# A two-layer encoder step: which MLP work runs plain, where the residual lives, and when the down operands are asked for

## The chip, the core and the metric

The kernel runs on one core of one Trainium2 chip. The core has a matrix engine (TensorE, PE in the profile), three other compute engines (VectorE or DVE, ScalarE or ACT, GpSimd or POOL), a sync engine (SP) from whose queue nearly all of this kernel's transfers are issued, and 16 DMA engines that carry them out. The metric is device time in microseconds (us) of one execution.

## The reference

The reference is one inference step of a two-layer encoder over 1024 prompt tokens and 32 sample tokens, 1056 rows of width 1024. Layer 0 mixes with a matrix memory, layer 1 with banded attention; each layer ends with the same kind of MLP. The change touches only what follows attention in layer 1:

```
x = layer_norm(ALPHA * x + (1 + g1) * y, ...)          # y: attention, projected
u = x * (1 + sc2) + sh2
f = square(relu(u @ w_up)) @ w_down                     # 1024 -> 4096 -> 1024
x = layer_norm(ALPHA * x + (1 + g2) * f, ...)
```

Everything is float32. The kernel carries each operand as a high and a low part and adds three products (high x high, high x low, low x high), so every matrix product costs three matmuls for each block of 128 inner rows. Making such a pair (`split`, line 90 with its cast on line 89) takes a cast on ScalarE and a subtraction on VectorE.

## The kernel before

Layer 1's MLP is `mlp7`, lines 1124 to 1515. The 1056 tokens are four quarters of 264 (`QN`). Two quarters make a token pair `tp`; `L.pairs` is (1, 0), so `tp0`, the first, is pair 1. The 4096 hidden columns are 16 groups of 256, here called pairs `pb`.

**Up, plain.** For the pairs listed in `FIRST` (10 to 15) the up product of the first token pair is made in the plain way: `up_tile` (24 matmuls of 264 columns, four of them, 96 in all, for a pair). Their weights come through `raw_up` transfers into a ring of three raw tiles and are split into `w_up`. The first three pairs run while the norm after attention still delivers the tokens, the other three behind them. When a pair's four tiles are done, pairs 14 and 15 go through `h_forms`; pairs 10 to 13 are only stored (`hraw`), and `late` reads them back and forms them later, in pieces laid beside the jobs.

**Up, seven products.** All other (pair, token pair) combinations, 26 of them, are jobs of `Seven`: seven products of 12 matmuls, 84 instead of 96, as in Strassen's scheme with Winograd's sums. They need seven weight forms (`forms`: 11 VectorE operations and 7 ScalarE casts of 128x512, made from two `rdn_u` loads) and moving forms of u (`tforms`: t1 and t2 in the TF tiles, t3 in `ext` and `exu`, T4 over a part of u that is no longer needed). A pair whose two token pairs both run this way (a double) shares its weight forms between two jobs; a pair of `FIRST` has one job only (a single). `seq` in `L1` gives the order: 0, 1, 10, 2, 3, 11, 4, 5, 12, 6, 7, 8, 9, 13, 14, 15.

**H forms.** `h_forms` squares a finished H tile and makes the seven forms that the down product wants: four in HL, three in HM, both single-buffered, stored to DRAM (`hd`). Pairs 14 and 15 are kept plain for the down side and stored to `hpl`.

**Down.** 20 units (five groups of 2 or 3 pairs, four output blocks each) of seven products, with weight forms from `rdn_d` and operands `fx` loaded back from `hd` into free rooms (`Rooms`, `fill`). `fill` asks for all operands for which there are rooms. Rooms come free late: the `ext` tile and half of u when the first token pair's last job is done, the H tiles' memory (the four `f4` tiles) and the rest of u after the last job. Pairs 14 and 15 follow plainly with operands `hs`, loaded from `hpl` into the `f4` tiles (line 1504).

**The residual.** `ACC` is one tile of 8 x 1056 columns. After the norm it is stored to DRAM (`xsp`), the TF tiles take its memory, and `L.reload(0..3)` brings it back in quarters around the end of the jobs; the down product adds into it (line 986).

**What sets the order.** TensorE's instructions in the jobs and the units stand in an order written out by hand (`manual_schedule`; product i of job j sorts by 7j + 2i, so neighbouring jobs interleave). The other engines' orders come from the Tile scheduler; SP's queue is one of them, and a transfer there waits behind any store that waits for its data.

Of the kernel before, what the change touches and what calls it, by code (L numbers as in the profile page):

```python
# [15 lines left out]
P = 128  # L16
# [59 lines left out]
def trunk_kernel(ctx: ExitStack, tc: tile.TileContext, a, o):  # L76
# [7 lines left out]
    def raw_tile(shape, name):  # L84
        return ring.tile(shape, F32, tag="raw", name=name, bufs=3)
# [1038 lines left out]
    def mlp7(L):  # L1124
# [11 lines left out]
        ep = e_cm.__enter__()  # L1136
        hraw = {pb: dr.tile([P, 4, QN], F32, name=f"hraw{l}_{pb}") for pb in L.first if pb < NW}
        hh_cm = tc.tile_pool(name=f"hh{l}", bufs=1, reuse_waits="tile")
# [17 lines left out]
        def h_place(pb, tp):  # L1156
            g = [i for i, (p0, kg) in enumerate(GRP) if p0 <= pb][-1]
            return hd[g][tp][:, :, pb - GRP[g][0]].rearrange("f p l t -> p f (l t)")

        def late(pb, tp):  # L1160

            H = raw_tile([P, 4, QN], f"hl_{l}_{pb}")
            nc.sync.dma_start(H, hraw[pb])
            yield
            dst = h_place(pb, tp)

            def put(f, src):
                t = tmp_t([P, 2, QN], f"hf_{l}_{pb}_{f}", F32R)
                split(t[:, 0], t[:, 1], src)
                nc.sync.dma_start(dst[:, f], t.bitcast(F32).rearrange("p l t -> p (l t)"))  # L1170
            nc.scalar.activation(H, H, AF.Square)
            put(B11, H[:, 1])
            put(B22, H[:, 2])
            yield
            put(B21, H[:, 3])
            nc.vector.tensor_sub(H[:, 1], H[:, 0], H[:, 1])
            nc.vector.tensor_sub(H[:, 0], H[:, 2], H[:, 0])
            put(T1, H[:, 1])
            yield
            nc.vector.tensor_sub(H[:, 2], H[:, 2], H[:, 1])  # L1180
            nc.vector.tensor_sub(H[:, 3], H[:, 3], H[:, 2])
            put(T3, H[:, 0])
            yield
            put(T2, H[:, 2])
            put(T4, H[:, 3])
            yield

# [199 lines left out]
        for j, pb in enumerate(rest):  # L1387
            for f in range(2):
                for q in L.quarters[:2]:
                    up_tile(pb, f, q)  # L1390
                if (j, f) == (0, 1):
                    L.ready(2)
                    tiles = L.scratch()
                    TF.update({(tp, i): tiles[2 * n + i] for n, tp in enumerate(L.pairs) for i in range(2)})
                    exts[tp1] = ring.tile([P, 2, KG, QN], F32R, tag="wc", name=f"exu_{l}", bufs=6)
                    tfs = [tf, tforms(tp1, exts[tp1])]
                if (j, f) == (1, 1):
                    prep(0)
                for n in ((), (0,), (1, 1), (0,), (0, 2), (2, 2))[2 * j + f]:
                    if n < 2:  # L1400
                        next(tfs[n])
# [5 lines left out]
        fx, nfx = {}, {}  # L1407
# [33 lines left out]

        next(tf, None)
        prep(1)
        got[0] = next(preps[0])
        for _ in tfs[1]:
            pass
        lone = max(j for j, (_, tp) in enumerate(jobs) if tp == tp0) + 1
        sevens, lates = {}, list(hraw)
        with tc.manual_schedule(engines={mybir.EngineType.PE}):
            for _, j, i in sorted((7 * j + 2 * i, j, i) for j in range(len(jobs)) for i in range(7)):  # L1450
# [4 lines left out]
                if tp == seq[n][1][-1]:  # L1455
                    advance(n, i)
                elif lates:
                    if i == 0:
                        job = late(lates[0], tp0)
                    if i < 5:  # L1460
                        next(job)
                    if i == 4:
                        del lates[0]
# [10 lines left out]
        for i in range(4):  # L1474
            rooms.add(f4p.tile([P, KG, 2, QN], F32R, tag=f"f4{i}", name=f"fx_4{i}_{l}"))
        for t in L.rooms(tp1):
            rooms.add(t)
        fill(0, fx)
        with tc.manual_schedule(engines={mybir.EngineType.PE}):
            for i, (g, m, phases) in enumerate(units):  # L1480
                more = g + 1 < len(GRP)
                if i < 3:
                    L.reload(i + 1)
                if i == 0:
# [376 lines left out]
    accp = acc_cm1.__enter__()  # L1861
    ACC = accp.tile([P, KC, T], F32, tag="acc", name="ACC")
    acc = {ti: ACC[:, :, t0:t0 + n] for ti, (t0, n) in enumerate(TBS)}
    acc["all"] = ACC
    for ti in rev:
        t0, n = TBS[ti]
        nc.sync.dma_start(acc[ti], xsp[1][:, :, t0:t0 + n])
        more_wo(ti)
# [22 lines left out]
    def end_out1(ti):  # L1891
        t0, n = TBS[ti]
        norms[ti] = flow.add(norm(ti, 2, f"n10_{ti}", W10[ti == rev[-1]], True, lambda ti: nc.sync.dma_start(
            xsp[2][:, :, t0:t0 + n], acc[ti])), now=NOW)
        qo_cm[ti].__exit__(None, None, None)
        if ti == 1:
            open_u2(0)
# [4 lines left out]
    wup1 = {}  # L1902
    FIRST = [10, 11, 12, 13, 14, 15]

# [7 lines left out]
    class L1:  # L1912
# [90 lines left out]
```

## Time and profile before

| | us |
|---|---|
| median of 3 runs | 2505.67 (2505.41 to 2506.22) |
| the profiled execution | 2506.99, its span 2505.2 |
| TensorE busy in the span | 2400.9 (96%) |
| VectorE busy | 1925.2 (77%) |
| ScalarE busy | 1090.4 (44%) |
| mean granted clock of TensorE | 0.980 of full speed |

The profile shows one execution. A row of a group gives line, engine, operation, output and inputs by the program's names, shapes and count, then busy time, the mean of one instruction in ns, and the idle time of the engine just before them with who ended it. The chain of waits is followed back from the last instruction. A table by stage gives the busy time of each engine in a stretch of the span. A timeline gives start and length in us. The up work of layer 1's MLP runs from about 1729 to 2117 us of the span, the down work from there to the end.

### The profile page before, as it was taken

To read this page: it belongs to the slowest core of one execution; us is meant where nothing else is said; L and a number is where in the kernel's file an instruction comes from. 1 tells how busy PE (TensorE), PEld (TensorE's weight loads), DVE (VectorE), ACT (ScalarE), POOL (GpSimd) and SP (SyncE) were. 2 spreads that over 40 slices of the span, in tenths; PEclk is the share of its full clock that TensorE was granted. 3 is DMA by queue.
4 is the path that set the end of the run, shared out by engine and by line. 5 is a ranking of instruction groups with operands and counts; after the bars stand their busy time and mean duration, and the time that the engine had idled before them with its cause. 6 is when DMAs were issued, how large, how long until landed. Compare 5 with 4: busy or idle time off the path is not lost.

```text
span 2505.2 us, 42905 instructions
## 1 busy us (share of the span) xinstructions
PE 2400.9 (96%) x16532; PEld 2307.3 (92%) x16532; DVE 1925.2 (77%) x4368; ACT 1090.4 (44%) x2280; POOL 166.6 (7%) x315
## 2 busy tenths in 40 slices
PE   8999999999999999999999899999978997899997
PEld 4999999999999999999999877799978997799997
DVE  4899999778778768766697766638978877677768
ACT  4544455481221221221375567736666665122212
POOL 0211100000000000000001244400000000000003
PEclk9999999999999999999999999999988999899999
DMA  8433224313223223223123400052567768856631
GB/s 294 120 108 100 83 90 131 99 35 118 93 86 125 93 93 119 93 93 115 59 94 96 101 1 1 25 139 82 167 213 280 262 239 310 326 217 224 234 125 70
DMA packets 248512, 335.29 MB, mean 134 GB/s; under 512 B 13032, under 2 KB 197756, under 8 KB 247284
## 3 DMA queue, kind: packets, MB, share of 16 engines
q1 hardware_dynamic: 248308, 332.55, 39.9%
q8 instruction: 130, 2.13, 0.3%
q14 instruction: 74, 0.61, 0.1%
HBM read 253.47 MB, written 81.40 MB: 134 GB/s over the span
## 4 chain that ended last, share of the span: by engine, by line
PE 74%; DVE 11%; DMA 5%; ACT 3%; issue 2%; POOL 1%; SPq 0%; ACTq 0%; DVEq 0%; POOLq 0%
PE dn L1433 11%; PE up L1333 7%; PE up L118 5%; PE up L119 5%; PE up L120 5%; PE dn L119 5%; PE dn L118 5%; PE dn L120 5%; PE pv L1771 3%; PE s L1714 2%; PE pt L1749 2%; PE o L118 1%; PE o L119 1%; PE o L120 1%; PE op_b L118 1%
## 5 line engine op out<-in xcount | busy, mean ns | idle before, releaser
L1433 PE MATMUL dn<-fx,wf_d 128*128 128x264 f32 x2016 | 257.3, 287 | 17.5 <-DMA fx<-hd 8.4
L1433 PEld LDWEIGHTS dn<-fx,wf_d 128*128 128x128 f32 x2016 | 252.3, 191 | 19.3 <-ACT wf_d L89 8.7
L119 PE MATMUL dn<-h,w_dn 128*128 128x384 f32 (+1 forms) x768 | 249.5, 325 | 0.0
L118 PE MATMUL up<-U,w_up 128*128 128x384 f32 (+1 forms) x768 | 249.2, 325 | 0.0
L119 PE MATMUL up<-U,w_up 128*128 128x384 f32 (+1 forms) x768 | 247.9, 323 | 0.0
L118 PE MATMUL dn<-h,w_dn 128*128 128x384 f32 (+1 forms) x768 | 247.8, 323 | 0.0
L120 PE MATMUL up<-U,w_up 128*128 128x384 f32 (+1 forms) x768 | 247.6, 322 | 0.0
L120 PE MATMUL dn<-h,w_dn 128*128 128x384 f32 (+1 forms) x768 | 247.3, 322 | 0.0
L986 DVE SCALAR_TENSOR_TENSOR ACC<-dn,ada,ACC 128x264 f32<-128x264 f32 (+5 forms) x400 | 160.5, 428 | 72.4 <-PE dn L1433 54.2
L238 DVE SCALAR_TENSOR_TENSOR aacc<-rada,cs,aacc 128x256 f32<-128x256 f32 x448 | 190.8, 481 | 0.0
L1333 PE MATMUL up<-u,wf_u 128*128 128x264 f32 x1248 | 170.5, 291 | 12.2 <-ACT wf_u L89 9.2
L1333 PEld LDWEIGHTS up<-u,wf_u 128*128 128x128 f32 x1248 | 162.4, 194 | 13.2 <-ACT wf_u L89 9.4
L986 DVE SCALAR_TENSOR_TENSOR acc<-dn,ada,acc 128x384 f32<-128x384 f32 (+2 forms) x256 | 119.9, 489 | 48.3 <-PE dn L120 46.7
L1025 ACT ACTIVATE r<-up 128x384 f32<-128x384 f32 (+1 forms) x96 | 44.5, 464 | 246.4 <-PE up L120 236.5
L119 PEld LDWEIGHTS dn<-h,w_dn 128*128 128x128 f32 x768 | 144.5, 188 | 0.2 <-DVE h L1028 0.2
L120 PEld LDWEIGHTS dn<-h,w_dn 128*128 128x128 f32 x768 | 144.5, 188 | 0.0
L120 PEld LDWEIGHTS up<-U,w_up 128*128 128x128 f32 x768 | 144.3, 188 | 0.0
L119 PEld LDWEIGHTS up<-U,w_up 128*128 128x128 f32 x768 | 144.2, 188 | 0.0
L118 PEld LDWEIGHTS up<-U,w_up 128*128 128x128 f32 x768 | 144.2, 188 | 0.1
L118 PEld LDWEIGHTS dn<-h,w_dn 128*128 128x128 f32 x768 | 143.9, 187 | 0.2
L1027 DVE TENSOR_TENSOR r<-r 128x384 f32<-128x384 f32 (+1 forms) x96 | 50.0, 523 | 103.1 <-ACT h L1026 102.5
L1333 PE MATMUL up<-TF,wf_u 128*128 128x264 f32 x624 | 93.2, 301 | 20.3 <-ACT wf_u L89 8.9
(393 smaller groups left out, 6419.9 us busy)
## 6 DMA issues: line engine op xcount, KB each, us to landing
rada<-in_w_ada_dram SPq DMA_DIRECT2D x64, 512.0 KB
hd<-HL SPq DMA_DIRECT2D x24, 1056.0 KB
fx<-hd SPq DMA_DIRECT2D x48, 528.0 KB
raw_up<-in_w_up_dram SPq DMA_DIRECT2D x44, 512.0 KB
hd<-HM SPq DMA_DIRECT2D x24, 792.0 KB
raw_dn<-in_w_down_dram SPq DMA_DIRECT2D x36, 512.0 KB
ada_room<-in_w_ada_dram SPq DMA_DIRECT2D x32, 512.0 KB
rdn_u<-in_w_up_dram SPq DMA_DIRECT2D x32, 512.0 KB
```

The costliest lines, as they stand in the source:

```text
L118: nc.tensor.matmul(ps, wh, mov(0, k), start=(k == 0), stop=False)
L119: nc.tensor.matmul(ps, wh, mov(1, k), start=False, stop=False)
L120: nc.tensor.matmul(ps, wl, mov(0, k), start=False, stop=(k == nk - 1))
L238: nc.vector.scalar_tensor_tensor(acc[:, cnd], raw[:, k], sc, acc[:, cnd], op0=ALU.mult, op1=ALU.add)
L986: nc.vector.scalar_tensor_tensor(xs, ps[:, off + o:off + o + mm_], gate[:, fc, cnd:cnd + 1], xs, op0=ALU.mult, op1=ALU.add)
L1025: nc.scalar.activation(r, ps[:, :n], AF.Relu)
L1027: nc.vector.tensor_mul(r, r, r)
L1333: nc.tensor.matmul(p, self.ws[w][:, wl, k], moving(f, tp, xl, k), start=first and k + n_ == 0, stop=k == 3 and n_ == 2, skip_group_check=n ...
L1433: nc.tensor.matmul(p, ws[w][:, wl, k], t[:, s0, xl], start=first and k + n_ == 0, stop=k == kg - 1 and n_ == 2, skip_group_check=not first)
L1714: nc.tensor.matmul(s[:, b, :w], qst, kk[i][:, g, k0 + j0:k0 + j0 + w], start=(i == 0), stop=(i == 1))
L1749: nc.tensor.transpose(pt[:kp, j - j0, pr * P:(pr + 1) * P], ps_[pr][:, j * P:j * P + kp], ident)
L1771: nc.tensor.matmul(pv[64 * e:64 * e + 64, :nq], V[:kp, vt0 + j, g * 64:(g + 1) * 64], pts[e][:kp, j, :nq], start=(j == 0), stop=(j == nt - 1))
```

## The change

`FIRST` becomes the ten pairs 6 to 15; the jobs of seven products become 22, and `seq` lays doubles and singles alternately: 0, 6, 1, 7, 2, 8, 3, 9, 4, 10, 5, 11, 14, 12, 15, 13. `hraw` and `late` go; every finished plain pair is formed at once by `h_forms`. The steps of `tforms` and of the first weight forms are laid over the longer plain stretch (`at`).

The residual is two tiles of four column blocks each (`acc0`, `acc1`; class `Halves` finds the part asked for), and its transfers are two instead of one. The TF tiles of the first token pair lie in `acc0`, those of the second in `acc1`, and each half is loaded back when its token pair's jobs no longer read it.

`fill` takes a limit: after the first token pair's last job it asks for one operand at products 0, 2 and 4 of each job, and the residual's quarters 0 and 1 are asked for at the ends of two of these jobs, quarter 2 after the last one, quarter 3 at the first unit. For the last two groups the rooms are sorted, so that the fourth group uses the `f4` tiles first and the fifth uses them last.

```diff
-        hraw = {pb: dr.tile([P, 4, QN], F32, ...) for pb in L.first if pb < NW}
-        def late(pb, tp):
-            ...
             if hts[pb, tp][1] == 4:
-                H = hts.pop((pb, tp))[0]
-                if pb in hraw:
-                    nc.sync.dma_start(hraw[pb], H[:, 0:4])
-                else:
-                    h_forms(pb, tp, H)
+                h_forms(pb, tp, hts.pop((pb, tp))[0])
...
-                    tiles = L.scratch()
-                    TF.update({(tp, i): tiles[2 * n + i] for n, tp in enumerate(L.pairs) for i in range(2)})
+                    for n, tp in enumerate(L.pairs):
+                        for i, t in enumerate(L.scratch(n)):
+                            TF[tp, i] = t
...
-                if (j, f) == (1, 1):
+                at = 2 * j + f - 2 * len(rest) + 14
+                if at == 11:
                     prep(0)
-                for n in ((), (0,), (1, 1), (0,), (0, 2), (2, 2))[2 * j + f]:
+                for n in {1: (1,), 2: (1,), 3: (1,), 4: (1,), 5: (1,), 6: (1,), 7: (0,), 8: (0,), 11: (0, 2),
+                          12: (2,), 13: (2, 0)}.get(at, ()):
...
-        def fill(g, into):
+        def fill(g, into, most=99):
             kg = GRP[g][1]
-            while want and len(rooms.free) >= kg:
+            if g >= len(GRP) - 2:
+                rooms.free.sort(key=lambda r: any(r[0] is t for t in f4s) == (g == len(GRP) - 1))
+            while want and len(rooms.free) >= kg and most:
+                most -= 1
                 tp, f = want.pop(0)
...
-                if j == lone - 1 and i == 6:
+                if j == lone and i == 6:
                     rooms.add(ep.tile([P, KG, 2, QN], F32R, tag="e", name=f"fx_e{l}"))
                     for t in L.rooms(tp0):
                         rooms.add(t)
-                    fill(0, fx)
-        L.reload(0)
+                if j > lone + 1:
+                    if i in (0, 2, 4):
+                        fill(0, fx, 1)
+                    elif i == 6 and j < lone + 4:
+                        L.reload(j - lone - 2)
+        L.reload(2)
...
-    ACC = accp.tile([P, KC, T], F32, tag="acc", name="ACC")
+    def acc_half(i, name):
+        return accp.tile([P, 4, T], F32, tag=f"acc{i}", name=f"{name}{i}")
+    def acc_dma(d, x, out=False):
+        for i in range(0, KC, 4):
+            p = [d[:, i:i + 4], x[:, i:i + 4]]
+            nc.sync.dma_start(*(p if out else reversed(p)))
+    acc = {"all": Halves([acc_half(i, "ACC") for i in range(2)])}
...
-    FIRST = [10, 11, 12, 13, 14, 15]
+    FIRST = [6, 7, 8, 9, 10, 11, 12, 13, 14, 15]
-        seq = [(pb, (0,) if pb > 9 else (1, 0)) for pb in (0, 1, 10, 2, 3, 11, 4, 5, 12, 6, 7, 8, 9, 13, 14, 15)]
+        seq = [(pb, (0,) if pb in FIRST else (1, 0)) for pb in (0, 6, 1, 7, 2, 8, 3, 9, 4, 10, 5, 11, 14, 12, 15, 13)]
...
-        def scratch():
-            t = accp.tile([P, 4, 2, KG, QN], F32R, tag="acc", name="TF")
-            return [[t[:, i, hl] for hl in range(2)] for i in range(4)]
+        def scratch(i):
+            t = accp.tile([P, 2, 2, KG, QN], F32R, tag=f"acc{i}", name=f"TF{i}")
+            return [[t[:, n, hl] for hl in range(2)] for n in range(2)]
         def reload(m):
-            if m == 0:
-                acc["all"] = accp.tile([P, KC, T], F32, tag="acc", name="ACC2")
-            nc.sync.dma_start(acc["all"][:, 2 * m:2 * m + 2], xsp[2][:, 2 * m:2 * m + 2])
+            i = m // 2
+            if m % 2 == 0:
+                acc["all"].tiles[i] = acc_half(i, "ACX")
+            k = m % 2 * 2
+            nc.sync.dma_start(acc["all"].tiles[i][:, k:k + 2], xsp[2][:, 4 * i + k:4 * i + k + 2])
```

More of the change, by code (lines that the diff above doesn't have):

```diff
@@ L1136, in mlp7 @@
         ep = e_cm.__enter__()
-        hraw = {pb: dr.tile([P, 4, QN], F32, name=f"hraw{l}_{pb}") for pb in L.first if pb < NW}
         hh_cm = tc.tile_pool(name=f"hh{l}", bufs=1, reuse_waits="tile")
@@ L1158, in h_place @@
             return hd[g][tp][:, :, pb - GRP[g][0]].rearrange("f p l t -> p f (l t)")
-        def late(pb, tp):
[L1162 to L1186, printed above, removed]
         def h_forms(pb, tp, H):
@@ L1439, in unit @@
                         step(i)
-        next(tf, None)
         prep(1)
         got[0] = next(preps[0])
[L1445 to L1448, printed above, removed]
+        lone = max(j for j, (_, tp) in enumerate(jobs) if tp == tp0)
+        sevens = {}
         with tc.manual_schedule(engines={mybir.EngineType.PE}):
@@ L1456, in mlp7 @@
                     advance(n, i)
[L1457 to L1463, printed above, removed]
-                if j == lone - 1 and i == 6:
+                if j == lone and i == 6:
                     rooms.add(ep.tile([P, KG, 2, QN], F32R, tag="e", name=f"fx_e{l}"))
@@ L1473, in mlp7 @@
         f4p = f4_cm.__enter__()
-        for i in range(4):
-            rooms.add(f4p.tile([P, KG, 2, QN], F32R, tag=f"f4{i}", name=f"fx_4{i}_{l}"))
+        f4s += [f4p.tile([P, KG, 2, QN], F32R, tag=f"f4{i}", name=f"fx_4{i}_{l}") for i in range(4)]
+        for t in f4s:
+            rooms.add(t)
         for t in L.rooms(tp1):
@@ L1481, in mlp7 @@
                 more = g + 1 < len(GRP)
-                if i < 3:
-                    L.reload(i + 1)
+                if i == 0:
+                    L.reload(3)
                 if i == 0:
@@ L1861, in trunk_kernel, with __init__, part, __getitem__ @@
     accp = acc_cm1.__enter__()
-    ACC = accp.tile([P, KC, T], F32, tag="acc", name="ACC")
-    acc = {ti: ACC[:, :, t0:t0 + n] for ti, (t0, n) in enumerate(TBS)}
-    acc["all"] = ACC
+    class Halves:
+        def __init__(self, tiles, t0=0, n=T):
+            self.tiles, self.t0, self.n = tiles, t0, n
+        def part(self, t0, n):
+            return Halves(self.tiles, self.t0 + t0, n)
+        def __getitem__(self, at):
+            if at[1] == slice(None):
+                return self.part(at[2].start, at[2].stop - at[2].start)
+            k, t = at[1], at[2] if len(at) > 2 else slice(0, self.n)
+            k0 = k.start if isinstance(k, slice) else k
+            i = k0 // 4
+            k = slice(k0 - 4 * i, k.stop - 4 * i) if isinstance(k, slice) else k - 4 * i
+            return self.tiles[i][:, k, self.t0 + t.start:self.t0 + t.stop]
+    def acc_half(i, name):
[5 more added lines that the diff above has]
+    acc = {"all": Halves([acc_half(i, "ACC") for i in range(2)])}
+    for ti, (t0, n) in enumerate(TBS):
+        acc[ti] = acc["all"].part(t0, n)
     for ti in rev:
         t0, n = TBS[ti]
-        nc.sync.dma_start(acc[ti], xsp[1][:, :, t0:t0 + n])
+        acc_dma(xsp[1][:, :, t0:t0 + n], acc[ti])
         more_wo(ti)
@@ L1892, in end_out1 @@
         t0, n = TBS[ti]
-        norms[ti] = flow.add(norm(ti, 2, f"n10_{ti}", W10[ti == rev[-1]], True, lambda ti: nc.sync.dma_start(
-            xsp[2][:, :, t0:t0 + n], acc[ti])), now=NOW)
+        norms[ti] = flow.add(norm(ti, 2, f"n10_{ti}", W10[ti == rev[-1]], True, lambda ti: acc_dma(
+            xsp[2][:, :, t0:t0 + n], acc[ti], True)), now=NOW)
         qo_cm[ti].__exit__(None, None, None)
```

4 lines of the change are left out of this document (2 added, 2 removed).

## The prediction

> **What bounds the kernel now.** First the page: who fills the span, and the chain of waits.
>
> ```profile
> PE 2400.9 (96%) x16532; PEld 2307.3 (92%) x16532; DVE 1925.2 (77%) x4368; ACT 1090.4 (44%) x2280; POOL 166.6 (7%) x315
> PE 74%; DVE 11%; DMA 5%; ACT 3%; issue 2%; POOL 1%; SPq 0%; ACTq 0%; DVEq 0%; POOLq 0%
> ```
>
> TensorE carries the kernel: an edit is worth what it takes from TensorE's instructions or from its gaps. The gaps near the change show in a table by stage: length, then busy time and instruction count (x) of PE, PEld, DVE, ACT and POOL, the granted clock, DMA share, GB/s.
>
> ```profile
> 1724.00:1807.00 83.00, 77.02 (x610) 76.17 (x609) 78.67 (x114) 58.30 (x102) 0.00 (x0) 0.98 0.47 156
> 1807.00:1850.00 43.00, 29.23 (x185) 28.21 (x186) 31.72 (x48) 19.36 (x35) 0.00 (x0) 0.76 0.51 175
> 1850.00:1940.00 90.00, 82.55 (x621) 80.96 (x620) 75.71 (x142) 64.57 (x118) 0.00 (x0) 0.92 0.78 275
> 1940.00:2090.00 150.00, 150.00 (x1234) 150.00 (x1233) 125.20 (x210) 102.43 (x174) 0.00 (x0) 1.00 0.76 266
> 2090.00:2117.00 27.00, 17.55 (x126) 17.03 (x125) 17.57 (x34) 14.56 (x28) 0.00 (x0) 0.81 0.71 257
> 2117.00:2162.00 45.00, 30.26 (x220) 28.81 (x219) 28.92 (x77) 9.93 (x22) 0.00 (x0) 0.86 1.00 372
> ```
>
> Busy shares mislead here (matmuls overlap and slow down after a gap), so I count matmuls. Their spacing comes from TensorE's timeline, one full job of 84 between two like rows; plain work begins, and down work begins, at the other rows.
>
> ```profile
> 1729.09 0.29 PE L118 MATMUL up<-u,w_up 128*128 128x264 f32 x1
> ...
> 1730.35 0.42 PE L118 MATMUL up<-u,w_up 128*128 128x264 f32 x1
> 1730.57 0.42 PE L119 MATMUL up<-u,w_up 128*128 128x264 f32 x1
> ```
>
> ```profile
> 1940.01 3.08 PE L1333 MATMUL up<-u,wf_u 128*128 128x264 f32 x24
> ...
> 1950.23 3.08 PE L1333 MATMUL up<-u,wf_u 128*128 128x264 f32 x24
> ```
>
> ```profile
> 2117.11 1.62 PE L1433 MATMUL dn<-fx_e,wf_d 128*128 128x264 f32 x12
> ```
>
> A job takes 10.22 us, a matmul 0.1217; right after a gap they come at 0.22. From 1729.09 the 6 plain pairs (6 x 96 = 576 matmuls, 70.1 us, and about 2.5 for the slow start and the norm's sums) end at 1801.7. The 26 jobs of seven products need 26 x 10.22 = 265.7 and would end at 2067.4. They end at 2117.1: **49.7 us are gaps**. By counts: 1807 to 1850 has room for 353 and ran 185 (20.4 us lost); 1850 to 1940 room for 740, ran 621 (14.5); 1940 to 2090 nothing; 2090 to 2117 room for 222, ran 126 (11.7); the rest, 3.1, lies before 1807. Then 2117 to 2162 loses 18 more. Who is waited for, in the waits of TensorE from 1715 to 1960 and from 1960 to 2165 (us, times, longest):
>
> ```profile
> PE up L1333 <- ACT wf_u L89: 8.9, 3, 7.1
> PE up L1333 <- ACT TF L89: 4.2, 1, 4.2
> PE up L1333 <- DVE wf_u L90: 3.2, 3, 1.6
> ```
>
> ```profile
> PE up L1333 <- ACT wf_u L89: 9.2, 1, 9.2
> PE dn L1433 <- DMA fx<-hd: 8.4, 1, 8.4
> PE dn L1433 <- DVE ACC L986: 5.6, 3, 4.6
> ```
>
> So the first gap is the seven products waiting for weight forms and TF, which VectorE (78.67 of 83 us busy) and ScalarE have not made when the plain work ends; the one at 2090 to 2117 waits for a late weight load, the last for down operands.
>
> **The change, part by part.** *TensorE.* Four pairs move from seven products to plain on the first token pair: +4 x 96 - 4 x 84 = +48 matmuls, **+5.8 us**. The floor without gaps: 960 plain x 0.1217 = 116.8, with the 2.5 up to 1848.4, then 22 jobs x 10.22 = 224.8, ends at 2073.2.
>
> *VectorE.* Gone with the late forming: 28 hf and 16 hl operations; 8 more w_up, 4 more HL, HM and 128x528, 4 fewer H additions come. Rows grouped by shape (1720 to 2120; busy us, mean ns):
>
> ```profile
> L90 DVE TENSOR_TENSOR HL<-H,HL 128x1056 fp32r<-128x1056 f32 x27 | 33.9, 1256 | 11.9 <-ACT HL L89 11.9
> L90 DVE TENSOR_TENSOR HM<-H,HM 128x792 fp32r<-128x792 f32 x24 | 23.5, 981 | 3.4 <-ACT HM L89 3.3
> L1199 DVE TENSOR_TENSOR H<-H 128x528 f32<-128x528 f32 x24 | 17.0, 708 | 18.1 <-ACT H L1190 18.1
> L90 DVE TENSOR_TENSOR w_up<-raw_up,w_up 128x1024 fp32r<-128x1024 f32 x10 | 12.2, 1220 | 0.8 <-ACT w_up L89 0.8
> L90 DVE TENSOR_TENSOR hf<-hl,hf 128x264 fp32r<-128x264 f32 x28 | 11.2, 429 | 3.1 <-ACT hf L89 3.0
> ```
>
> 8 x 1.22 + 4 x (1.26 + 0.98 + 0.71) - 4 x 0.43 - 44 x 0.43 = +0.9 us: the sum stays, the place changes. Counted along the new order, at the rate at which VectorE's instructions follow each other (about 0.07 us under these means), VectorE has 128 us of work from 1721.5 until the first pair's weight forms stand. In the old order this count put the end of the first T4 at 1721.5 + 83.4 = 1804.9; the timeline ends it at 1807.3.
>
> ```profile
> 1806.02 1.25 DVE L90 TENSOR_TENSOR u<-t,u 128x1056 fp32r<-128x1056 f32 x1
> ```
>
> So about 1852, against plain work that ends at 1848.4 or later: the forms and TF are ready about when TensorE wants them, and the gap of 20.4 + 3.1 us goes. What becomes late next:
>
> *Loads in the plain stretch.* Forming H directly puts stores on SP's queue between the weight loads: the second half of pair 11 is asked for only behind pair 9's HL store. VectorE reaches that HL after 70.8 us of its count (1792.3); the load took 4.9 us before (below), the cast and the subtraction 2.3: ready near 1800, and by VectorE's order 1804. TensorE, after 5.5 pairs, wants it at 1729.1 + 2.5 + 64.3 = 1795.9. Cost taken: **8 us**, VectorE's order being the nearest row; bounds 0 (SP is ahead of its order) and 13 (one more such load behind it). No gap hides it; it delays all that follows, since 1848.4 + 8 is past 1852.
>
> ```profile
> 1767.81 4.92 DMA raw_up<-in_w_up_dram
> ```
>
> *Steady jobs.* Doubles and singles now alternate. Three jobs hold 46 VectorE instructions; at 125.20 / 210 = 0.596 each from the row 1940 to 2090, 27.4 us in 30.7: 89%, where that row ran 83% without loss. ScalarE keeps its 68%. Cost taken **2 us**, by that row; bounds 0 and, at the loss of row 1850 to 1940 for 16 jobs, 14.5 / 90 x 164 = 26.
>
> *The last six jobs* (61.3 us) are all singles, and carry the new one-by-one loads. By the sizes
>
> ```profile
> hd<-HL SPq DMA_DIRECT2D x24, 1056.0 KB
> fx<-hd SPq DMA_DIRECT2D x48, 528.0 KB
> ...
> hd<-HM SPq DMA_DIRECT2D x24, 792.0 KB
> ...
> rdn_u<-in_w_up_dram SPq DMA_DIRECT2D x32, 512.0 KB
> ```
>
> by the new order of SP 5 x 1848 + 1056 + 10 x 528 + 6 x 512 + 4 x 1056 (residual quarters) = 22,872 KB, 381 GB/s; row 2117 to 2162 moved 372 with its engines 100% busy. So transfers are at their limit, 63.0 us against 61.3, and the last weights (pair 13) stand on SP behind pair 14's stores and a residual quarter. Cost taken **7 us**, between 1.7 and the old 11.7, nearer the old: the weight load is again last in line. The Trainium skill, "DMA: Bandwidth & Descriptors", Specifications, gives a lower ceiling, some 358 GB/s of HBM per core; by it the stretch would need 65.4 us, an estimate, and the sum be 2.4 us worse. The 372 measured over 45 us speaks against it.
>
> *Down operands, residual halves.* When the jobs end, 10 of the first unit's 14 operands are asked for instead of 6, and two residual quarters less are left; but the next loads queue behind the last pair's HL and HM stores (its VectorE work some 9 us after the end). SP's timeline before:
>
> ```profile
> 2078.64 3.79 SPq L1117 DMA_DIRECT2D fx<-hd  x6
> ...
> 2127.97 16.58 SPq L1117 DMA_DIRECT2D fx<-hd  x16
> ...
> 2147.17 4.43 SPq L1281 DMA_DIRECT2D rdn_d<-in_w_down_dram  x2
> ```
>
> The weights of unit 3 (2147.17) waited behind those 16 loads, and so they do now: 17 loads, 9,240 KB, 25 us at 372, mostly begin at end + 9 or later. Taken **-3 us** of the 8.4 and the rest; bounds -8 (the whole wait) and +3 (the stores land late). The residual's doubled transfers are extra issues (under 0.5 us each on SP, which mostly waits): 0, at most 2.
>
> *The end.* Sorting the rooms leaves three of the four plain operands hs, instead of two, to be loaded after the last unit. That wait was 3.2 us; a further 1056 KB is 2.9 us at 372, partly behind the first one's matmuls: **+1.5**, bounds 0 and 4.
>
> ```profile
> PE dn L118 <- DMA hs<-hpl: 3.2, 1, 3.2
> ```
>
> **Sum.** 2073.2 + 8 + 2 + 7 = 2090.2 against 2117.1: -26.9; -3 + 1.5: **-28.4**. Against the profiled execution's 2506.99 that is 2478.6; it stands 1.3 above the median of the runs, so 2477.
>
> **Rivals.** *(1) VectorE in order, slower than before.* At 89% any operand that ScalarE has late stops everything behind it; VectorE waited 16.9 us for ScalarE on the 128x528 subtraction and 10.7 on HL between 1850 and 2117 already, and in 1850 to 1940 an 84% busy VectorE lost TensorE 14.5 us. At that rate all 22 jobs lose 36: 2073.2 + 8 + 36 + 7 = 2124.2, +7.1, with -1.5 behind it 2512.6, median 2511. It decides from 30 us lost in the jobs (0.14 us per us), where the gain is gone. Against it: the 150 us without a gap, whose work has the same parts. The Trainium skill, "TensorE: Matmul & The Clock Gate", Part 1, says that ScalarE and VectorE are strict FIFO and only TensorE reorders, weight loads alone: it backs this mechanism; no row shows an overtaking.
>
> ```profile
> DVE H L1199 <- ACT H L1190: 16.9, 16, 3.4
> DVE wf_u L90 <- ACT wf_u L89: 12.1, 9, 3.8
> DVE HL L90 <- ACT HL L89: 10.7, 10, 4.7
> ```
>
> *(2) Plain work starves.* The loads of pairs 12 to 15 stand behind stores like pair 11's; if each is 5.5 us late, 4 x 5.5 more: 2499. For it: VectorE is full there. Against it: the order gives each later pair 6 us of slack by the count.
> *(3) The first gap only moves.* If idle waits put VectorE's count 15 us later (1867), TensorE waits there as before: 2492. Against it: 4.3 us of idle in 83 before.
> *(4) All of it hides.* 5 us of gaps in all, -8 at the operands: 2073.2 + 5 - 2117.1 - 8 = -46.9: 2459.
>
> **How the numbers follow.** Forecast 0.52, rival (1) 0.16, (2) 0.14, (3) 0.10, (4) 0.08. The range, 2457 to 2505, takes in (3), most of (2) and (4) and the bounds of the unknown costs where they don't all fall one way; it leaves out (1) and a little of the two. Within 0.2% (5 us, what a measurement tells from no change) are some of (1) and (2): 0.05; slower 0.14; faster 0.81.
>
> **What the new profile would show.** Plain work to 1850 to 1860 with one wait on w_up at pair 11 or 12; the clock near 1.00 where 1807 to 1850 had 0.76; no wait on TF; seven products begin at once and their job rows keep 10.22 apart; a wait for wf_u near the end, smaller than 9.2; down work starts near 2090, its wait for fx under 8.4. The forecast falls if job rows drift apart through the middle, if w_up waits come for several pairs, or if the down work starts later than 2105.

## The result, and the profile after

| | before | after |
|---|---|---|
| median, us | 2505.94 (2505.41 to 2509.28) | 2483.03 (2478.93 to 2485.01) |
| profiled execution, us | 2506.99 | 2478.93 |
| its span | 2505.2 | 2477.2 |

The ratio, of the means, is 0.9904, 95% interval 0.9887 to 0.9921: 24 us faster, 20 to 28; the medians differ by 22.9. The forecast was 2477, and its sum, made against the profiled executions, 2478.6; the profiled execution took 2478.93, but it is the fastest of four, and the median stands 4 us above it. So the sum fits the traces better than it fits the median.

The page after: TensorE's busy time falls 9.7 us, and its share of the chain rises from 74% to 79%, while DMA's falls from 5% to 2%.

```profile
PE 2391.2 (97%) x16580; PEld 2300.1 (93%) x16580; DVE 1921.3 (78%) x4340; ACT 1090.5 (44%) x2264; POOL 167.9 (7%) x315
PE 79%; DVE 10%; ACT 2%; DMA 2%; issue 2%; POOL 0%; SPq 0%; DVEq 0%; ACTq 0%; POOLq 0%
```

The table by stage, with its columns as in the prediction; the stages are cut where this kernel's work changes.

```profile
1724.00:1807.00 83.00, 76.32 (x582) 75.64 (x582) 80.91 (x122) 61.00 (x102) 0.00 (x0) 0.94 0.59 202
1807.00:1860.00 53.00, 52.12 (x426) 51.75 (x425) 48.84 (x55) 35.79 (x54) 0.00 (x0) 1.00 0.76 253
1860.00:1940.00 80.00, 80.00 (x660) 80.00 (x659) 67.42 (x116) 54.22 (x95) 0.00 (x0) 1.00 0.65 225
1940.00:2060.00 120.00, 120.00 (x989) 120.00 (x988) 106.07 (x181) 88.78 (x153) 0.00 (x0) 1.00 0.83 290
2060.00:2090.00 30.00, 21.56 (x156) 20.87 (x154) 19.09 (x36) 15.71 (x29) 0.00 (x0) 0.83 0.79 279
2090.00:2135.00 45.00, 31.04 (x229) 29.68 (x228) 31.03 (x79) 11.37 (x27) 0.00 (x0) 0.85 0.98 363
```

From 1807 to 2060 TensorE runs almost without a gap, at a clock of 1.00: the second row has room for 436 matmuls and ran 426. Before, the stretch 1807 to 1850 ran 185 of 353 at 0.76. The gaps left are in the last two rows: 156 of 246 (11.0 us lost) and 229 of 370 (17.2 us). TensorE's timeline gives their ends and what ended them. (ACX, in the rows that follow, is the residual's tile when it is loaded back, ACC before.)

```profile
1855.21 3.11 PE L1300 MATMUL up<-u,wf_u 128*128 128x264 f32 x24
```

```profile
2074.48 3.30 PE L1300 MATMUL up<-u,wf_u 128*128 128x264 f32 x12 [8.04 <-ACT wf_u L89]
...
2092.87 1.61 PE L1300 MATMUL up<-u,wf_u 128*128 128x264 f32 x12
...
2113.21 5.06 PE L1406 MATMUL dn<-fx,wf_d 128*128 128x264 f32 x24 [12.01 <-DMA fx<-hd]
```

The seven products begin at 1855.21, 0.12 us behind the last plain matmul. The last one ends at 2094.3 with 21 down matmuls (2.6 us) already between; without these the jobs would end at 2091.7.

### The profile page after: what moved, and what is told of

Same layout as the page of the kernel before. It is cut to its first block, busy times and chain, and to the rows that moved or that the text cites. A ratio compares the mean times of both kernels' runs of the same rounds, so it can differ in the third digit from the quotient of the medians.

```text
span 2477.2 us, 42903 instructions
## 1 busy us (share of the span) xinstructions
PE 2391.2 (97%) x16580; PEld 2300.1 (93%) x16580; DVE 1921.3 (78%) x4340; ACT 1090.5 (44%) x2264; POOL 167.9 (7%) x315
## 4 chain that ended last, share of the span: by engine, by line
PE 79%; DVE 10%; ACT 2%; DMA 2%; issue 2%; POOL 0%; SPq 0%; DVEq 0%; ACTq 0%; POOLq 0%
PE dn L1406 11%; PE up L1300 8%; PE up L120 6%; PE up L118 6%; PE up L119 6%; PE dn L119 5%; PE dn L118 5%; PE dn L120 5%; PE pv L1739 3%; PE s L1682 2%; PE pt L1717 2%; PE op_a L118 1%; PE op_a L119 1%; PE op_a L120 1%; PE o L118 1%
## 5 line engine op out<-in xcount | busy, mean ns | idle before, releaser
L1406 PEld LDWEIGHTS dn<-fx,wf_d 128*128 128x128 f32 x2016 | 250.0, 189 | 18.5 <-DMA fx<-hd 12.2
L986 DVE SCALAR_TENSOR_TENSOR ACX<-dn,ada,ACX 128x264 f32<-128x264 f32 (+5 forms) x400 | 160.1, 427 | 66.7 <-PE dn L1406 47.5
L1300 PE MATMUL up<-u,wf_u 128*128 128x264 f32 x1056 | 140.9, 286 | 8.5 <-ACT wf_u L89 8.0
L1300 PEld LDWEIGHTS up<-u,wf_u 128*128 128x128 f32 x1056 | 133.8, 189 | 9.3 <-ACT wf_u L89 8.2
L89 ACT CAST w_up<-raw_up 128x1024 fp32r<-128x1024 f32 x52 | 54.3, 1047 | 140.3 <-DMA raw_up<-in_w_up_dram 122.6
```

Source lines behind the costliest of these rows:

```text
L89: nc.scalar.copy(dst_h, src)
L986: nc.vector.scalar_tensor_tensor(xs, ps[:, off + o:off + o + mm_], gate[:, fc, cnd:cnd + 1], xs, op0=ALU.mult, op1=ALU.add)
L1300: nc.tensor.matmul(p, self.ws[w][:, wl, k], moving(f, tp, xl, k), start=first and k + n_ == 0, stop=k == 3 and n_ == 2, skip_group_check=n ...
L1406: nc.tensor.matmul(p, ws[w][:, wl, k], t[:, s0, xl], start=first and k + n_ == 0, stop=k == kg - 1 and n_ == 2, skip_group_check=not first)
```

## Experiments

All times are medians; ratios are against the kernel before, run beside each. "The changed kernel" is the 2483.03 of above.

### six_direct: late forming alone

```diff
-        hraw = {pb: dr.tile([P, 4, QN], F32, ...) for pb in L.first if pb < NW}
+        hraw = {}
```

> The kernel before, its six pairs kept, with pairs 10 to 13 formed at once and no late forming. Theory A (VectorE's queue is full while the plain work runs, and the longer plain stretch is what pays): four pairs' H forms, 4 x 3.6 = 14 us of VectorE work, now lie ahead of the first weight forms, so the gap at 1800 to 1850 grows from 23 us to 30 or more, the 14.5 us lost from 1850 to 1940 shrink to under 8, and the time is 2500 to 2514 us. Rival B (late forming is what made the gaps, ten pairs aren't needed): the first gap keeps its 23 us, the loss from 1850 to 1940 goes, and the time is near 2490.

Measured: 2495.83, ratio 0.9960 (0.9946 to 0.9974), 10 us faster than before. Its table by stage:

```profile
1724.00:1807.00 83.00, 75.23 (x578) 74.99 (x579) 79.99 (x120) 60.27 (x103) 0.00 (x0) 0.94 0.58 195
1807.00:1850.00 43.00, 30.35 (x195) 28.49 (x194) 37.98 (x50) 21.96 (x34) 0.00 (x0) 0.80 0.40 129
1850.00:1940.00 90.00, 90.00 (x741) 90.00 (x741) 76.31 (x128) 63.24 (x109) 0.00 (x0) 1.00 0.71 248
```

From 1850 to 1940 it ran 741 matmuls where the kernel before ran 621: the 14.5 us are gone with late forming. Up to 1850 it ran 773 against 795, 2.7 us worse. So theory A's first gap stays, as it said, but grows by far less than the 7 us expected, and rival B is right for the second stretch; the time lies between the two expectations and inside neither. Of the whole gain some 10 of 23 us come from dropping late forming; ten pairs and the rest bring the other 13.

### eight: how many pairs

```diff
-    FIRST = [6, 7, 8, 9, 10, 11, 12, 13, 14, 15]
+    FIRST = [8, 9, 10, 11, 12, 13, 14, 15]
-        seq: 0, 6, 1, 7, 2, 8, 3, 9, 4, 10, 5, 11, 14, 12, 15, 13
+        seq: 0, 8, 1, 9, 2, 10, 3, 11, 4, 12, 5, 6, 7, 14, 15, 13
-                for n in {1: (1,), 2: (1,), 3: (1,), 4: (1,), 5: (1,), 6: (1,), 7: (0,), 8: (0,), 11: ...
+                for n in {5: (1,), 6: (1, 1), 7: (0, 1), 8: (0, 1), 9: (1,), 11: ...
```

> The changed kernel with eight pairs plain (8 to 15) and 24 jobs, doubles and singles alternating as far as the singles reach, the steps of the moving forms laid closer. Theory A (plain work must last as long as VectorE needs for TF and the first forms, about 128 us of work): plain work would end near 1831 to 1835 and VectorE be ready near 1842, so 7 to 12 us of gap come back, 2.9 us of matmuls are saved; time 2486 to 2493. Rival B (late forming was all, the pair count does not matter): no gap, time 2478 to 2482. Rival C (it falls back to the six-pair figure): 2494 to 2498.

Measured: 2489.52, ratio 0.9931 (0.9916 to 0.9946). The stage that decides:

```profile
1807.00:1860.00 53.00, 44.50 (x335) 42.64 (x335) 44.42 (x53) 29.59 (x45) 0.00 (x0) 0.97 0.56 182
```

335 of 436 matmuls, 12.3 us lost, against 1.2 with ten pairs. The time is theory A's: the plain stretch has to be as long as VectorE needs. The waits are only in part where it put them. TensorE's waits from 1800 to 1862:

```profile
PE up L120 <- DVE w_up L90: 3.9, 2, 2.2
PE up L118 <- ACT w_up L89: 1.8, 2, 1.4
```

Most of the 8.4 us of waits there, these 5.7, is for plain weights inside the plain stretch, which ends at 1840.5 instead of the expected 1831 to 1835; the jobs begin right behind it and wait 1.1 us for weight forms, 1.6 for ScalarE's copies into H, and not for TF. VectorE makes both kinds of weights and is busy 80.98 of the 83 us up to 1807, so shorter plain work waits for it inside the stretch instead of behind it.

### raw_pool: where pair 11's weights wait

```diff
-            nc.sync.dma_start(dst, src)
+            (nc.gpsimd if name[:3] == "up1" else nc.sync).dma_start(dst, src)
```

> The changed kernel with the plain weights of layer 1 (raw_up) asked for on GpSimd's queue instead of SP's. Theory A (pair 11's weights are late because their load stands behind pair 9's HL store on SP): TensorE's waits on w_up of pair 11, 4.7 us and 7.5 us with the slow clock after them, go; plain work ends near 1849 instead of 1855, and the seven products start at most 3 us behind it; the time falls by 4 to 7 us. Rival B (VectorE and ScalarE make w_up late in their own order, whatever the load does): the wait stays above 3 us. Rival C (the first weight forms become the wait instead, VectorE having no slack): plain work ends early, but the jobs begin at the same time as now, and the time stays within 2 us.

Measured: 2489.71, ratio 0.9935 (0.9920 to 0.9950), 7 us slower than the changed kernel. GpSimd's timeline has the two loads of pair 11 at 1765 and 1775; SP had issued them at 1784 and 1790.

```profile
1765.52 0.75 POOL L96 DMA_DIRECT2D raw_up<-in_w_up_dram  x1 [7.42 <-DVE H L1173]
1775.18 0.75 POOL L96 DMA_DIRECT2D raw_up<-in_w_up_dram  x1 [8.90 <-DVE ext L90]
```

TensorE and ScalarE of the same kernel, where the first wait is for pair 11's first half:

```profile
1794.73 0.39 PE L118 MATMUL up<-u,w_up 128*128 128x264 f32 x1 [3.84 <-ACT w_up L89]
...
1797.18 0.59 PE L120 MATMUL up<-u,w_up 128*128 128x264 f32 x1 [1.16 <-DVE w_up L90]
```

```profile
1792.66 1.08 ACT L1161 ACTIVATE H<-H 128x1056 f32<-128x1056 f32 x1
1793.65 1.98 ACT L89 CAST w_up<-raw_up 128x1024 fp32r<-128x1024 f32 x2
```

With the 4.9 us that such a load took before, the weights were there by 1780, 14 us ahead of their cast, and TensorE waited all the same: ScalarE casts them where they stand in its order, behind H forms and the norm, and VectorE follows. That is rival B. SP's queue is not what held pair 11. The changed kernel has the same wait, with 1.19 us at 1793.63 for the subtraction behind it, and there too ScalarE goes to this cast without a wait for the load:

```profile
1790.11 1.03 ACT L89 CAST w_up<-raw_up 128x1024 fp32r<-128x1024 f32 x1
1791.19 0.39 PE L118 MATMUL up<-u,w_up 128*128 128x264 f32 x1 [2.59 <-ACT w_up L89]
```

The 7 us that GpSimd's queue costs lie elsewhere: 35 matmuls fewer from 1724 to 1860 (971 for 1006, 4.3 us) and 23 fewer from 1860 to 1940 (637 for 660, 2.8 us). The scheduled engines' orders differ there; why was not taken apart.

### tail_light: nothing asked for during the jobs

```diff
-                if j > lone + 1:
-                    if i in (0, 2, 4):
-                        fill(0, fx, 1)
-                    elif i == 6 and j < lone + 4:
-                        L.reload(j - lone - 2)
-        L.reload(2)
+        for m in range(3):
+            L.reload(m)
```

> The changed kernel with no down operand and no residual quarter asked for during the jobs: all of them come after the last job. Theory A (the last weight load is late because the transfers are at their limit from 2045 on): the load for pair 13 lands 4 to 5 us after its issue instead of 8.7, TensorE's wait of 8.0 for weight forms falls to about 3.5, and the jobs end some 5 us earlier; the down operands then cost more than the 12.0 us they cost now, 10 operands and 2 quarters (7.4 MB, 20 us at 372 GB/s) more behind the end, so the time is 2488 to 2498. Rival B (it is late because SP issues it behind pair 14's stores): landing and wait stay within 1 us of 8.7 and 8.0, and the time is 2495 to 2503.

Measured: 2483.79, ratio 0.9911 (0.9891 to 0.9931): no change of the time. TensorE's timeline:

```profile
2076.40 3.09 PE L1300 MATMUL up<-u,wf_u 128*128 128x264 f32 x24
2079.33 1.62 PE L1406 MATMUL dn<-fx_e,wf_d 128*128 128x264 f32 x12
...
2089.40 4.30 PE L1406 MATMUL dn<-fx,wf_d 128*128 128x264 f32 x18 [4.72 <-DMA fx<-hd]
2100.28 1.66 PE L1406 MATMUL dn<-fx,wf_d 128*128 128x264 f32 x6 [6.58 <-DMA fx<-hd]
2104.06 1.69 PE L1406 MATMUL dn<-fx,wf_d 128*128 128x264 f32 x6 [2.12 <-DMA fx<-hd]
```

Both expectations missed the time. The wait for weight forms is gone altogether, not halved, and the jobs end 12 us earlier; but the down work gives all of it back in three waits for operands and one of 5.2 us for the residual. SP's timeline, first of the changed kernel, then of this one, shows why the run doesn't part theory A from rival B:

```profile
2061.67 2.71 SPq L1167 DMA_DIRECT2D hpl<-HL  x4
...
2065.09 1.45 SPq L1248 DMA_DIRECT2D rdn_u<-in_w_up_dram  x2
```

```profile
2054.03 0.38 SPq L1248 DMA_DIRECT2D rdn_u<-in_w_up_dram  x1
...
2057.34 0.37 SPq L1248 DMA_DIRECT2D rdn_u<-in_w_up_dram  x1
```

The last weights (pair 13) now stand ahead of pair 14's stores (here at 2059.51), 9 to 11 us earlier, and that earlier place in the queue could do by itself what theory A expects of fewer transfers. That the time comes out even could mean that from 2045 to 2135 one sum of transfers has to pass, and that taking it out of one place puts it into the next; u2_first speaks against that.

### one_tile: the residual in one tile again

```diff
-        return accp.tile([P, 4, T], F32, tag=f"acc{i}", name=f"{name}{i}")
+        if i == 0:
+            whole.append(accp.tile([P, KC, T], F32, tag="acc", name=name))
+        return whole[-1][:, 4 * i:4 * i + 4]
```

(and TF in one tile in the same way, the four quarters asked for behind the jobs and at the first three units)

> The changed kernel with the residual in one tile again, TF in one tile, and so all four residual quarters asked for after the last job, as before; ten plain pairs and one-by-one operands stay. Theory A (with ten pairs plain, TF has time enough, and the transfers saved in the jobs come back behind them): no wait on TF where the seven products begin, and the time within 3 us of 2483. Rival B (the two halves carry part of the gain, since a TF part no longer waits for the whole residual's store): TensorE waits 4 us or more on TF or weight forms near 1855, and the time is 2487 or more.

Measured: 2480.71, ratio 0.9905 (0.9886 to 0.9923). Theory A: the half tiles and the early quarters, which this edit takes back together, bring nothing that can be measured. TensorE's waits from 1715 to 1870 name neither TF nor weight forms; from 2080 to 2145 they are

```profile
PE dn L1406 <- DMA fx<-hd: 13.7, 2, 13.5
PE dn L1406 <- DVE ACX L986: 3.0, 1, 3.0
```

and the wait for weights before them is 3.0 us instead of 8.0 (put down to wf_d, a down form): again one wait for another.

### fill_all: operands all at once

```diff
                     for t in L.rooms(tp0):
                         rooms.add(t)
+                    fill(0, fx)
                 if j > lone + 1:
-                    if i in (0, 2, 4):
-                        fill(0, fx, 1)
-                    elif i == 6 and j < lone + 4:
+                    if i == 6 and j < lone + 4:
```

> The changed kernel with all ten early down operands asked for at once behind the first token pair's last job, as before, instead of one at products 0, 2 and 4; the residual's quarters stay where they are. Theory A (the transfers from 2045 to 2135 are one full queue, and asking one by one only changes who waits in it): the wait for the last weight forms (8.0 us) moves by up to 3 us either way, the wait for operands (12.0 us) by as much the other way, and the time stays within 3 us of 2483. Rival B (one by one is what lets the weights through): the weights wait 12 us or more and the time is 2487 or more.

Measured: 2488.43, ratio 0.9934 (0.9911 to 0.9956), 5 us slower than the changed kernel. Theory A's 3 us are passed; rival B has the time right, but TensorE waits for the weights of the pair two ahead of the last, and in all 9.6 us, not 12. SP's timeline, and TensorE's waits from 1870 to 2096:

```profile
2032.21 3.68 SPq L1117 DMA_DIRECT2D fx<-hd  x6
...
2042.81 1.90 SPq L1248 DMA_DIRECT2D rdn_u<-in_w_up_dram  x2
```

```profile
PE up L1300 <- ACT wf_u L89: 9.6, 2, 8.9
PE up L1300 <- DVE H L1306: 4.2, 2, 3.9
```

Six operands stand in one piece where the changed kernel asks for weights (at 2032.94); the weights go out 10 us later. Asking one by one is worth some 5 us here.

### last15: the last two jobs swapped

```diff
-        seq: ..., 11, 14, 12, 15, 13
+        seq: ..., 11, 14, 12, 13, 15
```

> The changed kernel with the last two jobs swapped (13, then 15), so that the pair formed last needs no HL and HM store ahead of the down operands, only the four plain stores. Theory A (the wait of 12.0 us for down operands is SP holding 15 loads behind the last HM store, issued 9 us after the jobs): the loads go out 5 us or more earlier, the wait falls to 5 to 8, the time to 2476 to 2480 (profile 2473 to 2476). Rival B (the transfers are full anyway, 98% busy there): the wait stays within 2 us of 12.0 and the time within 3 us of 2483.

Measured: 2480.53, ratio 0.9900 (0.9885 to 0.9916); the wait for operands is 12.2 us, unchanged. By its numbers that is rival B. But SP's timeline shows the 15 loads again behind stores, now the four plain stores of pair 15:

```profile
2103.29 2.55 SPq L1167 DMA_DIRECT2D hpl<-HL  x4
2105.89 15.29 SPq L1117 DMA_DIRECT2D fx<-hd  x15
```

So it did not take the suspected cause away, and tells nothing against theory A. The next run does.

### u2_first: other rooms for the first unit's operands

```diff
-        for t in f4s:
-            rooms.add(t)
         for t in L.rooms(tp1):
             rooms.add(t)
+        for t in f4s:
+            rooms.add(t)
         fill(0, fx)
```

> The changed kernel with the rooms that come free at the end of the jobs offered in the other order: first those in the memory of u (free with the last matmul of the jobs), then those in the memory of the H tiles (free only when the last pair's HL and HM stores have landed). Nothing else moves; the first unit's last four operands now go into u's memory, three of them ahead of those stores on SP's queue. Theory A (the 12.0 us for down operands are paid because these four wait for rooms behind the last H stores): the loads go out near 2095 instead of 2104, the wait falls to 5 or less, and the time to 2473 to 2478. Rival B (between 2045 and 2135 the transfers are full, so whatever is asked for earlier delays something else, as when the operands were taken out of the jobs, which moved the waits and not the time): the wait moves to another operand or to weights, and the time stays within 3 us of 2483.

Measured: 2474.43, ratio 0.9873 (0.9859 to 0.9888), 9 us faster than the changed kernel. SP's timeline, and TensorE's waits from 2080 to 2145:

```profile
2093.29 1.60 SPq L1117 DMA_DIRECT2D fx<-hd  x3
2098.53 0.37 SPq L1172 DMA_DIRECT2D hd<-HL  x1
```

```profile
PE dn L1406 <- DVE ACX L986: 8.8, 3, 5.8
PE dn L1406 <- DMA fx<-hd: 4.4, 1, 4.4
```

Theory A: the operands go out at 2093 instead of 2104, ahead of the last HL store, and the wait falls from 12.0 to 4.4. Rival B keeps a part: the waits for the adds into the residual grow from 2.3 to 8.8. The wait for hs at the end is gone too. So the transfers from 2045 to 2135 are not one full sum: a load that gets a buffer sooner does gain time.

### nosort and u2_nosort: the sorting of the rooms

```diff
-            if g >= len(GRP) - 2:
-                rooms.free.sort(key=lambda r: any(r[0] is t for t in f4s) == (g == len(GRP) - 1))
```

> The changed kernel without the sorting of the rooms for the last two groups. Theory A (sorting only decides which plain operands hs are late at the end): the wait for hs falls from 4.9 us to 3.2 as before, nothing else moves, the time falls by 1 to 2 us, less than the runs scatter. Rival B (sorting brings operands of the last group earlier): waits for fx of 1 us or more appear in the units after 2135, and the time rises.

Measured: 2478.37, ratio 0.9889 (0.9871 to 0.9906). TensorE's wait of this kind from 2145 on, in the changed kernel and in this one:

```profile
PE dn L118 <- DMA hs<-hpl: 4.9, 1, 4.9
```

```profile
PE dn L118 <- DMA hs<-hpl: 2.3, 1, 2.3
```

The wait for hs falls from 4.9 to 2.3 us, and no waits for fx come: theory A, as far as the profile goes. That the median fell by 4.7 is more than this wait, and within the scatter of the runs (2475 to 2482).

With u2_first's edit and this one together:

> The changed kernel with both edits that each shortened a wait: u's memory offered first for the first unit's last operands (2474.4 us by itself), and no sorting of the rooms for the last groups. If the two waits are separate, in time and in cause, the operands' wait stays near 4.4, the hs wait is 3.2 or less, and the time is 2471 to 2475. If the sorting's loss was only that hs waits behind the H tiles' rooms, which u's memory first has already removed (no hs wait stands in that kernel's waits), the time stays at 2473 to 2477 and the sorting is worth nothing either way.

Measured: 2473.82, ratio 0.9878 (0.9854 to 0.9902), the shortest median of all. Against u2_first's 2474.43 that is no difference. The time lies in both expected ranges; what speaks for the second reading is that u2_first alone has no wait for hs any more, so that there was none left for this edit to remove.

### u2_reload and u2_1415: two attempts on what is left

Both start from u2_nosort. The first moves the residual's quarters:

```diff
-                    elif i == 6 and j < lone + 4:
-                        L.reload(j - lone - 2)
-        L.reload(2)
+        for m in range(3):
+            L.reload(m)
```

> The kernel with the rooms in the order u's memory, then H's (2474.4 us), without the sorting, and with the residual's quarters 0 and 1 asked for after the last job too. Theory A (2.1 MB less in the jobs let the last weight load through, as with one residual tile, where the wait for weights was 3.0; the down side has room for them, since its first adds come some us later): the wait for weights falls from 8.0 to about 3, no new wait over 4 us comes, and the time is 2466 to 2471. Rival B (the queue is full up to 2135, what is saved ahead is paid behind, as when everything was taken out of the jobs): waits on the residual or on operands grow by what the weights gain, and the time is 2472 to 2477.

The second changes the order of the last jobs:

```diff
-        seq: ..., 11, 14, 12, 15, 13
+        seq: ..., 11, 12, 13, 14, 15
```

> The same without the quarters' move (u's memory first, no sorting, quarters as in the changed kernel), and the jobs' order ending 12, 13, 14, 15: the last two pairs are stored plain, so the last HL and HM stores lie two jobs ahead of the end. Theory A (what is left of the operands' wait, 4.4 us, and of the adds' waits after it come from the last pair's forming and stores): down work loses 3 to 5 us less, time 2468 to 2472. Rival B (full transfers): within 2 us of the 2472 to 2474 that u's memory first gives without sorting.

Measured: 2476.69, ratio 0.9890 (0.9866 to 0.9914), and 2479.59, ratio 0.9899 (0.9875 to 0.9922). In the first the wait for weights falls to 1.5 us, but 3.0 for the H additions, 9.5 for the residual and 6.3 for operands stand beside it (u2_nosort: 0.4, 9.0 and 4.4): rival B. In the second the wait for weights grows to 9.1, with 8.8 for the residual; its time is above both expectations, and why was not followed up.

## Why the prediction was right, and where it was not

*The floor and the sum.* With 10.22 us a job it put the end of the jobs at 2090.2; they ended at 2091.7, 25.4 us earlier than before, for 26.9 forecast. From there to the end of the span went 385.5 us instead of 388.1: 2.6 gained for 1.5. Together 28.0 for 28.4, between the profiled executions; between the medians it is 22.9. That the sum is so near is in part luck. Ahead of the end of the jobs two terms were too large by 3.2 us together and one too small by 4.7. Behind it the two terms come to a loss of 0.4 where a gain of 1.5 was forecast, and 3.0 us are gained in the later units and the plain end, for which the sum has no term.

*The first gap.* "The forms and TF are ready about when TensorE wants them": the seven products began at 1855.21, with no wait. The count put the first pair's weight forms at about 1852; in VectorE's timeline the last of the forms made from sums ends at 1851.8:

```profile
1849.27 2.49 DVE L90 TENSOR_TENSOR wf_u<-s_u,wf_u 128x512 fp32r<-128x512 f32 x4
```

Rival (3) did not come. Run eight shows what shorter plain work costs.

*The stretch 1850 to 1940.* Here a cause was missed, and that the forecast holds all the same is luck. The prediction gives these 14.5 us no cause of their own: its floor of 2073.2 drops them with the other gaps, rival (1) reads them as the loss of a busy VectorE, and late forming is priced only by the VectorE time that it takes (+0.9 in all). Six_direct keeps the short plain work and takes only late forming away, and the 14.5 us go, with VectorE as busy as before (76.31 of 90 us for 75.71). So it was not the amount of VectorE's work. Waits of VectorE and ScalarE from 1850 to 1940, in the kernel before, then in six_direct:

```profile
DVE wf_u L90 <- ACT wf_u L89: 5.8, 3, 3.8
ACT hl L1171 <- DMA hl<-hraw: 1.6, 1, 1.6
```

```profile
DVE wf_u L90 <- ACT wf_u L89: 0.8, 1, 0.8
```

In the kernel before, VectorE waits for ScalarE's casts of weight forms, ScalarE waits for a late piece that is read back, and neither waits there for a weight load. That speaks for the late pieces' place in the two orders; no run separates it from their transfers.

*Loads in the plain stretch.* 8 us forecast; the plain work ended 6.8 us behind its floor. The size was near, the mechanism wrong: the step "the second half of pair 11 is asked for only behind pair 9's HL store" names SP's queue, but raw_pool has the weights 14 us early and the wait stays. The wait is not even for that half: SP does ask for it behind the HL store (1789.86), but TensorE waits for the first half (1791.19 and 1793.63 above), and for the second not at all. What was right is the other row, VectorE's order (and ScalarE's).

*Steady jobs.* 2 us forecast, none measured: from 1860 to 2060 TensorE ran 1646 matmuls, all that these 200 us have room for. VectorE was busy 173.48 of them (87%, for 89% counted). Rival (1) did not come. The strict first in, first out of ScalarE and VectorE that it takes from the Trainium skill ("TensorE: Matmul & The Clock Gate", Part 1) needs an operand that comes late; no wait of TensorE in these 200 us names one.

*The last six jobs.* This is the term that was mis-sized: 7 us forecast, 11.7 lost (8.4 of waits and the slow clock behind them). The place of the last weights was read rightly: pair 13's stand behind pair 14's stores and a residual quarter (2065.09, shown at tail_light). The volume was not. The first row below has the whole stretch: 308 GB/s at a share of 0.88, about 18.9 MB, where the sum has 22,872 KB (23.4 MB). Four operands had been asked for ahead of it, one quarter came behind it, and fewer stores fell into it than were counted. The transfers were at their limit only in a part of it, the second row; in the third they have little to do.

```profile
2030.40:2091.70 61.30, 52.81 (x411) 51.96 (x410) 47.04 (x82) 40.67 (x73) 0.00 (x0) 0.92 0.88 308
2045.00:2075.00 30.00, 21.56 (x173) 21.12 (x171) 21.75 (x36) 19.09 (x32) 0.00 (x0) 0.90 1.01 351
2080.00:2090.00 10.00, 10.00 (x84) 9.95 (x82) 6.09 (x16) 5.44 (x11) 0.00 (x0) 1.00 0.35 106
```

In the third row SP waits 6.5 us before it can ask for residual quarter 2, until the last product that reads TF in that memory is done. 351 GB/s at a share of 1.01 is less than the 372 that the sum used. The figure of the Trainium skill ("DMA: Bandwidth & Descriptors", Specifications, some 358 GB/s of HBM per core), set aside there because a row had 372, would have made the term 9.4, an estimate: nearer, but by the same volume. The rows here lie on both sides of that figure (351, and 363 from 2090 to 2135).

*Down operands.* The sign of the wait was wrong. "Taken -3 us of the 8.4": the wait grew to 12.0. The prediction saw that the loads queue behind the last HL and HM stores, and still counted 10 operands asked for early, instead of 6, as the larger effect. But they were 10 before as well: SP's timeline of the kernel before has four more ahead of the six that the prediction shows.

```profile
2062.92 0.34 SPq L1117 DMA_DIRECT2D fx_e<-hd  x1
...
2067.91 0.48 SPq L1117 DMA_DIRECT2D fx_e<-hd  x1
2068.81 1.91 SPq L1117 DMA_DIRECT2D fx<-hd  x2
```

Nor did it see that the last four are given rooms in the H tiles' memory, which those very stores have to leave first (u2_first). The stage as a whole lost 17.2 us for 18 before, since waits on the residual's adds shrank from 5.6 to 2.3. So a gain of 1 stands where 3 was forecast (1.3, counted to the same matmul in both, at 2175.55 and 2148.81).

*The end.* 1.5 forecast; the hs wait went from 3.2 to 4.9, and nosort takes it back.

*Rivals (2) and (4)* did not come: no w_up wait past pair 12 was over 1 us, and both late waits stayed.

## What to carry to other kernels

When a busy engine prepares operands for the bound one, count its work along its own emitted order up to the operand that is wanted first: it told within a few us how long the covering work has to be. Work laid beside the bound engine's jobs can cost more than the time that it takes on the engine that does it, as late forming did here. Taking transfers out of one stretch (tail_light) moved the waits and not the time, though the transfers were not full throughout; look for the load that waits for a buffer, not only for bandwidth. Which buffer a load is given decides what it has to wait for, and a change of that order alone was worth some 9 us here.

## What the runs showed of the hardware

The limit of the transfers is not one number: 351 GB/s over 30 us (2045 to 2075) and 363 over 45 (2090 to 2135) at shares of 1.01 and 0.98 in one kernel, with 408 in a single stretch of 10 us:

```profile
2115.00:2125.00 10.00, 10.00 (x75) 0.91 1.02 408
```

By SP's timeline stores and loads are mixed differently in these stretches; what sets the rate was not tried.
